# A batched inner product: larger loads, another order of the loads, and a new way of giving them to the two queues

## The chip, the cores and the metric

The kernel runs on one core of one Trainium2 chip. The metric is the device time in microseconds (us): the median of three runs of the kernel before was 49.61 us (49.56 to 49.82). The profile is of a single execution; its span, 47.8 us, leaves out a little of what the device time counts.

## The reference

Two inputs of 32 matrices each are multiplied element by element, and each product is summed to one number:

```python
x, y: (32, 256, 256) float32
return np.einsum('bij,bij->b', x, y).astype(np.float32)   # 32 numbers
```

Each input is 8.39 MB, so 16.78 MB have to be read once; the output is 128 bytes.

## The kernel before

A matrix has 65,536 elements, 512 for each of the 128 partitions (`F = 512`). The kernel reads the inputs as a flat row of numbers and cuts it in blocks of three sizes. A **single** is one matrix (256 KB for x, rows of 2 KB in each partition). A **pair** is two matrices (512 KB, rows of 4 KB): the first 64 partitions hold the first one. A **slab** is four matrices (1 MB, rows of 8 KB), 32 partitions for each. At the end there are **halves** of a single: half of the columns (128 KB, rows of 1 KB). Each block is loaded twice, once from x and once from y.

The order in the program is: singles 0 and 1, pair 1, slabs 1 to 4, pairs 10 to 14, then matrices 30 and 31 in two halves each. A function per size (`load_single`, `load_pair`, `load_slab`, `load_half`) takes the next of two DMA queues in turn, SyncE's (`nc.sync`, SP in the profile, queue q1) and ScalarE's (`nc.scalar`, ACT, queue q10), issues the load of x and then of y on it, and calls `ttr`.

`ttr` (line 81) is one VectorE instruction that multiplies the two tiles, throws the products away into `junk`, and sums each partition's products into one column of an accumulator: `acc_slab`, `acc_pair` or `acc_one`. A short second instruction reads the accumulated value out. The second half of a matrix begins with the sum of the first half (`chain=True`).

The sum over partitions is left to TensorE: a matmul of the accumulator with a mask of ones for the right partitions (lines 142, 158 and 175). VectorE copies each result from PSUM to SBUF (lines 150, 166, 177), and small transfers bring it to the output (line 151 for slabs, 167 and 170 for pairs, 178 and 179 for singles and halves).

The framework orders the work. Each tile pool gives its buffers out in turn (`SLAB_BUFS = 4`, `PAIR_BUFS = 4`, `SM_BUFS = 6`), and a load into a buffer in use waits until VectorE has read it. Loads also take eight completion semaphores, DMAHW0 to DMAHW7, in turn; a load waits on its queue until the transfer that last used its semaphore has landed. Each queue issues its transfers in order, so a load that waits holds up the loads behind it.

Of the kernel before, what the change touches and what calls it, by code (L numbers as in the profile page):

```python
# [9 lines left out]
SLAB = 4  # L10
SLAB_BUFS = 4
PAIR_BUFS = 4
SM_BUFS = 6


@with_exitstack
def kernel(
    ctx: ExitStack,
    tc: tile.TileContext,
    x: bass.AP,  # L20
    y: bass.AP,
    out: bass.AP,
):
    nc = tc.nc
    P = nc.NUM_PARTITIONS

    B, M, N = x.shape
    E = M * N
    F = E // P

    x_flat = x.rearrange("b i j -> (b i j)")
    y_flat = y.rearrange("b i j -> (b i j)")

    def grouped(flat, nb):
        return flat.rearrange("(u p f) -> u p f", p=P, f=nb * F)

    x_slab = grouped(x_flat, SLAB)
    y_slab = grouped(y_flat, SLAB)
    x_pair = grouped(x_flat, 2)
    y_pair = grouped(y_flat, 2)  # L40
    x_one = grouped(x_flat, 1)
    y_one = grouped(y_flat, 1)

    n_slabs = 4
    n_pairs = 6
    assert 2 + 2 + n_slabs * SLAB + 5 * 2 + 2 == B

    slab_pool = ctx.enter_context(tc.tile_pool(name="slab", bufs=SLAB_BUFS))
    pair_pool = ctx.enter_context(tc.tile_pool(name="pair", bufs=PAIR_BUFS))
    sm_pool = ctx.enter_context(tc.tile_pool(name="sm", bufs=SM_BUFS))  # L50
    singles_pool = ctx.enter_context(tc.tile_pool(name="singles", bufs=1))
    psum_pool = ctx.enter_context(tc.tile_pool(name="psum", bufs=1, space=bass.MemoryType.PSUM))

    acc_slab = singles_pool.tile([P, n_slabs], mybir.dt.float32)
    acc_pair = singles_pool.tile([P, n_pairs], mybir.dt.float32)
    acc_one = singles_pool.tile([P, 4], mybir.dt.float32)
    junk = singles_pool.tile([P, SLAB * F], mybir.dt.float32)

    lanes = P // SLAB
    mask_slab = singles_pool.tile([P, SLAB], mybir.dt.float32)  # L60
    nc.vector.memset(mask_slab[:], 0.0)  # L61
    for q in range(SLAB):
        nc.vector.memset(mask_slab[q * lanes : (q + 1) * lanes, q : q + 1], 1.0)  # L63
    mask_pair = singles_pool.tile([P, 2], mybir.dt.float32)
    nc.vector.memset(mask_pair[:], 0.0)
    nc.vector.memset(mask_pair[0:64, 0:1], 1.0)
    nc.vector.memset(mask_pair[64:128, 1:2], 1.0)
    ones = singles_pool.tile([P, 1], mybir.dt.float32)
    nc.vector.memset(ones[:], 1.0)

    rings = [nc.sync, nc.scalar]
    ring_idx = 0

    def next_ring():
        nonlocal ring_idx
        eng = rings[ring_idx % 2]
        ring_idx += 1
        return eng

    def ttr(x_ap, y_ap, acc_ap, chain=False):  # L80
        nc.vector.tensor_tensor_reduce(  # L81
            out=junk[:, : x_ap.shape[-1]],
            in0=x_ap,
            in1=y_ap,
            scale=1.0,
            scalar=(acc_ap if chain else 0.0),
            op0=mybir.AluOpType.mult,
            op1=mybir.AluOpType.add,
            accum_out=acc_ap,
        )  # L90

    def load_single(b, col):
        eng = next_ring()
        x_tile = sm_pool.tile([P, F], mybir.dt.float32, name="x_s")
        y_tile = sm_pool.tile([P, F], mybir.dt.float32, name="y_s")
        eng.dma_start(out=x_tile[:], in_=x_one[b])
        eng.dma_start(out=y_tile[:], in_=y_one[b])
        ttr(x_tile[:], y_tile[:], acc_one[:, col : col + 1])

    def load_half(b, h, col, chain):  # L100
        H = F // 2
        eng = next_ring()
        x_tile = sm_pool.tile([P, H], mybir.dt.float32, name="x_h")
        y_tile = sm_pool.tile([P, H], mybir.dt.float32, name="y_h")
        eng.dma_start(out=x_tile[:], in_=x_one[b][:, h * H : (h + 1) * H])
        eng.dma_start(out=y_tile[:], in_=y_one[b][:, h * H : (h + 1) * H])
        ttr(x_tile[:], y_tile[:], acc_one[:, col : col + 1], chain=chain)

    def load_pair(u, col):
        eng = next_ring()  # L110
        x_tile = pair_pool.tile([P, 2 * F], mybir.dt.float32, name="x_p")
        y_tile = pair_pool.tile([P, 2 * F], mybir.dt.float32, name="y_p")
        eng.dma_start(out=x_tile[:], in_=x_pair[u])
        eng.dma_start(out=y_tile[:], in_=y_pair[u])
        ttr(x_tile[:], y_tile[:], acc_pair[:, col : col + 1])

    def load_slab(u, col):
        eng = next_ring()
        x_tile = slab_pool.tile([P, SLAB * F], mybir.dt.float32, name="x_b")
        y_tile = slab_pool.tile([P, SLAB * F], mybir.dt.float32, name="y_b")  # L120
        eng.dma_start(out=x_tile[:], in_=x_slab[u])
        eng.dma_start(out=y_tile[:], in_=y_slab[u])
        ttr(x_tile[:], y_tile[:], acc_slab[:, col : col + 1])

    load_single(0, 0)
    load_single(1, 1)
    load_pair(1, 0)
    for i in range(n_slabs):
        load_slab(1 + i, i)
    load_pair(10, 1)  # L130
    load_pair(11, 2)
    load_pair(12, 3)
    load_pair(13, 4)
    load_pair(14, 5)
    load_half(30, 0, 2, False)
    load_half(30, 1, 2, True)
    load_half(31, 0, 3, False)
    load_half(31, 1, 3, True)

    res_slab_psum = psum_pool.tile([n_slabs, SLAB], mybir.dt.float32)  # L140
    for q in range(SLAB):
        nc.tensor.matmul(  # L142
            res_slab_psum[:, q : q + 1],
            acc_slab[:],
            mask_slab[:, q : q + 1],
            start=True,
            stop=True,
        )
    res_slab_sbuf = singles_pool.tile([n_slabs, SLAB], mybir.dt.float32)
    nc.vector.tensor_copy(out=res_slab_sbuf[:], in_=res_slab_psum[:])  # L150
    nc.sync.dma_start(
        out=out[4 : 4 + n_slabs * SLAB].rearrange("(c q) -> c q", q=SLAB),
        in_=res_slab_sbuf[:],
    )

    res_pair_psum = psum_pool.tile([n_pairs, 2], mybir.dt.float32)
    for g in range(2):
        nc.tensor.matmul(  # L158
            res_pair_psum[:, g : g + 1],
            acc_pair[:],  # L160
            mask_pair[:, g : g + 1],
            start=True,
            stop=True,
        )
    res_pair_sbuf = singles_pool.tile([n_pairs, 2], mybir.dt.float32)
    nc.vector.tensor_copy(out=res_pair_sbuf[:], in_=res_pair_psum[:])  # L166
    nc.scalar.dma_start(
        out=out[2:4].rearrange("(c g) -> c g", g=2), in_=res_pair_sbuf[0:1]
    )
    nc.scalar.dma_start(  # L170
        out=out[20:30].rearrange("(c g) -> c g", g=2), in_=res_pair_sbuf[1:6]
    )

    res_one_psum = psum_pool.tile([4, 1], mybir.dt.float32)
    nc.tensor.matmul(res_one_psum[:], acc_one[:], ones[:], start=True, stop=True)  # L175
    res_one_sbuf = singles_pool.tile([4, 1], mybir.dt.float32)
    nc.vector.tensor_copy(out=res_one_sbuf[:], in_=res_one_psum[:])  # L177
    nc.sync.dma_start(out=out[0:2], in_=res_one_sbuf[0:2, 0])
    nc.sync.dma_start(out=out[30:32], in_=res_one_sbuf[2:4, 0])


# [28 lines left out]
```

## Time and profile before

| what | value |
|---|---|
| time, median of 3 | 49.61 us |
| span of the profiled execution | 47.8 us |
| moved by DMA | 16.79 MB, mean 351 GB/s |
| VectorE busy | 20.6 us (43%), 44 instructions |
| TensorE busy | 0.8 us (2%) |
| ScalarE busy with computing | none |
| product of a slab, pair, single, half | 2.29, 1.23, 0.69, 0.43 to 0.49 us |
| issue of the last load; of the last output | 42.07; 45.69 us |

The page shows the span in 40 slices of 1.19 us each; a digit is the busy share of a slice in tenths. A line of the timeline begins with the start in us and the duration, then engine, line, operation and tiles; engines with a q (SPq, ACTq) are the queues' issuing instructions. A line of the stretches has the busy time and count of instructions of TensorE, its weight load, VectorE and GpSimd, then TensorE's clock, the DMA share and GB/s.

### The profile page before, as it was taken

Reading aid. Unit: us, or ns where it says so; the run is one execution under the profiler, and the core shown is the slowest. Engines: PE = TensorE matmul, PEld = TensorE weight load, DVE = VectorE, ACT = ScalarE, POOL = GpSimd, SP = SyncE. Lnnn points to the kernel's source line nnn. Section 1 sums busy time; section 2 is a strip of 40 time slices with the busy share of each in tenths; the row PEclk is TensorE's granted clock in tenths of the full one; section 3 lists DMA queues with packets and bytes.
Section 4 is the critical chain, followed back from the end, with each engine's and each line's share of the span. In section 5 each row is a group of like instructions: output and inputs, shape, how many; then the busy total and the mean of one; then the engine's idle time right before and its main releaser. Section 6 shows DMA issues by size and latency. Waiting matters only on the chain.

```text
span 47.8 us, 176 instructions
## 1 busy us (share of the span) xinstructions
PE 0.8 (2%) x14; PEld 0.5 (1%) x14; DVE 20.6 (43%) x44; POOL 0.2 (0%) x4
## 2 busy tenths in 40 slices
PE   0000000000000000000000000002000000001100
PEld 0000000000000000000000000002000000001000
DVE  2100005051900494008901970899254549199700
POOL 1000000000000000000000000000000000000000
DMA  0689999999999999999999999999999999994000
GB/s 0 103 285 434 381 417 412 415 443 432 418 418 412 412 432 439 419 412 432 412 408 436 391 439 395 405 412 412 401 422 391 424 395 398 354 323 119 0 0 7
DMA packets 4637, 16.79 MB, mean 351 GB/s; under 512 B 540, under 2 KB 1564, under 8 KB 3612
## 3 DMA queue, kind: packets, MB, share of 16 engines
q10 hardware_dynamic: 2316, 8.39, 44.9%
q1 hardware_dynamic: 2320, 8.39, 44.2%
q14 instruction: 1, 0.01, 0.0%
HBM read 16.78 MB, written 0.00 MB: 351 GB/s over the span
## 4 chain that ended last, share of the span: by engine, by line
DMA 84%; issue 5%; DVE 4%; PE 0%
DMA y_b<-in_y_dram 33%; DMA x_p<-in_x_dram 28%; DMA y_p<-in_y_dram 12%; DMA x_s<-in_x_dram 11%; DVE junk L81 3%; DVE acc_one L81 1%; PE res_one_psum L175 0%; DVE res_one_sbuf L177 0%; DVE acc_pair L81 0%; DVE res_pair_sbuf L166 0%
## 5 line engine op out<-in xcount | busy, mean ns | idle before, releaser
L81 DVE CUSTOM_DVE_ANT_0 junk<-x_b,y_b 128x2048 f32<-128x2048 f32 x4 | 9.2, 2292 | 10.1 <-DMA y_b<-in_y_dram 6.9
L81 DVE CUSTOM_DVE_ANT_0 junk<-x_p,y_p 128x1024 f32<-128x1024 f32 x6 | 7.4, 1225 | 5.6 <-DMA y_p<-in_y_dram 4.5
L81 DVE CUSTOM_DVE_ANT_0 junk<-x_s,y_s 128x512 f32<-128x512 f32 x2 | 1.4, 692 | 7.7 <-DMA y_s<-in_y_dram 7.7
L81 DVE CUSTOM_DVE_ANT_0 junk<-x_h,y_h,acc_one 128x256 f32<-128x256 f32 x2 | 1.0, 485 | 0.0
L81 DVE CUSTOM_DVE_ANT_0 junk<-x_h,y_h 128x256 f32<-128x256 f32 x2 | 0.9, 426 | 0.1
L142 PE MATMUL res_slab_psum<-mask_slab,acc_slab 128*4 128x1 f32 x8 | 0.3, 164 | 32.4 <-DVE acc_slab L81 32.4
L142 PEld LDWEIGHTS res_slab_psum<-mask_slab,acc_slab 128*4 128x4 f32 x8 | 0.2, 83 | 32.4 <-DVE acc_slab L81 32.4
L81 DVE DVE_READ_ACCUMULATOR2_ANT acc_pair<- 128x1 f32 x6 | 0.5, 83 | 0.0
L81 DVE DVE_READ_ACCUMULATOR2_ANT acc_one<- 128x1 f32 x6 | 0.5, 83 | 0.0
L158 PE MATMUL res_pair_psum<-mask_pair,acc_pair 128*6 128x1 f32 x4 | 0.2, 164 | 10.2 <-DVE acc_pair L81 10.2
L61 DVE MEMSET mask_slab<- 128x4 f32 x1 | 0.1, 62 | 0.8 <-PEq L194 0.8
L81 DVE DVE_READ_ACCUMULATOR2_ANT acc_slab<- 128x1 f32 x4 | 0.3, 82 | 0.0
L63 DVE MEMSET mask_slab<- 32x1 f32 x4 | 0.2, 59 | 0.1
L177 DVE COPY res_one_sbuf<-res_one_psum 4x1 f32<-4x1 f32 x1 | 0.1, 145 | 0.3 <-PE res_one_psum L175 0.3
L158 PEld LDWEIGHTS res_pair_psum<-mask_pair,acc_pair 128*6 128x6 f32 x4 | 0.1, 86 | 10.3 <-DVE acc_pair L81 10.3
L175 PE MATMUL res_one_psum<-ones,acc_one 128*4 128x1 f32 x2 | 0.2, 165 | 1.8 <-DVE acc_one L81 1.8
L150 DVE COPY res_slab_sbuf<-res_slab_psum 4x4 f32<-4x4 f32 x1 | 0.1, 145 | 0.0
L166 DVE COPY res_pair_sbuf<-res_pair_psum 6x2 f32<-6x2 f32 x1 | 0.1, 143 | 0.0
L175 PEld LDWEIGHTS res_one_psum<-ones,acc_one 128*4 128x4 f32 x2 | 0.1, 84 | 1.9 <-DVE acc_one L81 1.9
L194 POOL MEMSET const-bfloat16-1.0<- 128x1 bf16 x1 | 0.1, 101 | 0.0
L194 POOL MEMSET const-uint8-127<- 128x1 uint8 x1 | 0.1, 101 | 0.0
L194 POOL MEMSET const-float32-0.0<- 128x1 f32 x1 | 0.1, 98 | 0.2 <-issue 0.2
(5 smaller groups left out, 0.3 us busy)
## 6 DMA issues: line engine op xcount, KB each, us to landing
x_b<-in_x_dram ACTq DMA_DIRECT2D x2, 1024.0 KB, 5.6
x_b<-in_x_dram SPq DMA_DIRECT2D x2, 1024.0 KB, 13.7
y_b<-in_y_dram SPq DMA_DIRECT2D x2, 1024.0 KB, 18.2
y_b<-in_y_dram ACTq DMA_DIRECT2D x2, 1024.0 KB, 9.7
x_p<-in_x_dram SPq DMA_DIRECT2D x3, 512.0 KB, 16.4
y_p<-in_y_dram SPq DMA_DIRECT2D x3, 512.0 KB, 9.5
x_p<-in_x_dram ACTq DMA_DIRECT2D x3, 512.0 KB, 13.1
y_p<-in_y_dram ACTq DMA_DIRECT2D x3, 512.0 KB, 15.6
```

The costliest lines, as they stand in the source:

```text
L61: nc.vector.memset(mask_slab[:], 0.0)
L63: nc.vector.memset(mask_slab[q * lanes : (q + 1) * lanes, q : q + 1], 1.0)
L81: nc.vector.tensor_tensor_reduce(out=junk[:, : x_ap.shape[-1]], in0=x_ap, in1=y_ap, scale=1.0, scalar=(acc_ap if chain else 0.0), op0=mybi ...
L142: nc.tensor.matmul(res_slab_psum[:, q : q + 1], acc_slab[:], mask_slab[:, q : q + 1], start=True, stop=True,)
L150: nc.vector.tensor_copy(out=res_slab_sbuf[:], in_=res_slab_psum[:])
L158: nc.tensor.matmul(res_pair_psum[:, g : g + 1], acc_pair[:], mask_pair[:, g : g + 1], start=True, stop=True,)
L166: nc.vector.tensor_copy(out=res_pair_sbuf[:], in_=res_pair_psum[:])
L175: nc.tensor.matmul(res_one_psum[:], acc_one[:], ones[:], start=True, stop=True)
L177: nc.vector.tensor_copy(out=res_one_sbuf[:], in_=res_one_psum[:])
L194: nc = _bacc.Bacc("TRN2", target_bir_lowering=False, num_devices=1)
```

## The change

The change loads most of the input in the largest block. The inputs are cut in six slabs (matrices 0 to 23), two pairs (24 to 27), two singles (28 and 29) and the four halves as before (30 and 31), in this order from large to small, so that the small pieces stand at the end and little work is left after the last one. Blocks are given to the queue that has fewer bytes so far (`pick_ring`), with the first two slabs fixed to one queue each; the function for these is called `load_slab_quarters`, but it loads whole slabs just as `load_slab` does. The copies of the slab and pair results from PSUM move from VectorE to ScalarE, and the outputs, now in one piece for each accumulator, need one transfer each: three in place of five. `SM_BUFS` goes from 6 to 8. The masks, the products and the matmuls are the same.

In the built program SyncE's queue has slabs 0, 2 and 4, and ScalarE's slabs 1, 3 and 5, then one pair, one single and two halves each. ScalarE's two copies, with a load of its function table ahead of the first, stand behind all loads of its queue. SyncE's queue ends with the slab output, which waits for the first of these copies, and the output of singles and halves. SyncE's loads use the even semaphores and ScalarE's the odd ones.

```diff
-SM_BUFS = 6
+SM_BUFS = 8
...
-    acc_slab = singles_pool.tile([P, n_slabs], mybir.dt.float32)
-    acc_pair = singles_pool.tile([P, n_pairs], mybir.dt.float32)
+    n_slab_cols = 6
+    acc_slab = singles_pool.tile([P, n_slab_cols], mybir.dt.float32)
+    acc_pair = singles_pool.tile([P, 2], mybir.dt.float32)
...
-    def next_ring():
-        nonlocal ring_idx
-        eng = rings[ring_idx % 2]
-        ring_idx += 1
-        return eng
+    ring_bytes = [0, 0]
+
+    def pick_ring(nbytes, forced=None):
+        if forced is None:
+            i = 0 if ring_bytes[0] <= ring_bytes[1] else 1
+        else:
+            i = forced
+        ring_bytes[i] += nbytes
+        return rings[i]
...
+    def load_slab_quarters(u, col, ring_i):
+        eng = pick_ring(2 * FS * P * 4, forced=ring_i)
+        x_tile = slab_pool.tile([P, FS], mybir.dt.float32, name="x_b")
+        y_tile = slab_pool.tile([P, FS], mybir.dt.float32, name="y_b")
+        eng.dma_start(out=x_tile[:], in_=x_slab[u])
+        eng.dma_start(out=y_tile[:], in_=y_slab[u])
+        ttr(x_tile[:], y_tile[:], acc_slab[:, col : col + 1])
...
-    load_single(0, 0)
-    load_single(1, 1)
-    load_pair(1, 0)
-    for i in range(n_slabs):
-        load_slab(1 + i, i)
-    load_pair(10, 1)
-    load_pair(11, 2)
-    load_pair(12, 3)
-    load_pair(13, 4)
-    load_pair(14, 5)
+    load_slab_quarters(0, 0, 0)
+    load_slab_quarters(1, 1, 1)
+    load_slab(2, 2)
+    load_slab(3, 3)
+    load_slab(4, 4)
+    load_slab(5, 5)
+    load_pair(12, 0)
+    load_pair(13, 1)
+    load_single(28, 0)
+    load_single(29, 1)
     load_half(30, 0, 2, False)
     load_half(30, 1, 2, True)
     load_half(31, 0, 3, False)
     load_half(31, 1, 3, True)
...
-    nc.vector.tensor_copy(out=res_slab_sbuf[:], in_=res_slab_psum[:])
+    nc.scalar.copy(out=res_slab_sbuf[:], in_=res_slab_psum[:])
     nc.sync.dma_start(
-        out=out[4 : 4 + n_slabs * SLAB].rearrange("(c q) -> c q", q=SLAB),
+        out=out[0 : n_slab_cols * SLAB].rearrange("(c q) -> c q", q=SLAB),
         in_=res_slab_sbuf[:],
     )
...
-    nc.vector.tensor_copy(out=res_pair_sbuf[:], in_=res_pair_psum[:])
+    nc.scalar.copy(out=res_pair_sbuf[:], in_=res_pair_psum[:])
     nc.scalar.dma_start(
-        out=out[2:4].rearrange("(c g) -> c g", g=2), in_=res_pair_sbuf[0:1]
-    )
-    nc.scalar.dma_start(
-        out=out[20:30].rearrange("(c g) -> c g", g=2), in_=res_pair_sbuf[1:6]
+        out=out[24:28].rearrange("(c g) -> c g", g=2), in_=res_pair_sbuf[:]
     )
...
-    nc.sync.dma_start(out=out[0:2], in_=res_one_sbuf[0:2, 0])
-    nc.sync.dma_start(out=out[30:32], in_=res_one_sbuf[2:4, 0])
+    nc.sync.dma_start(out=out[28:32], in_=res_one_sbuf[:, 0])
```

## The prediction

> **What bounds the kernel now.** I read the page's slices first, for the limiting resource.
>
> ```profile
> span 47.8 us, 176 instructions
> DVE  2100005051900494008901970899254549199700
> DMA  0689999999999999999999999999999999994000
> ```
>
> From slice 3 (3.6 us) to slice 35 (43.0 us) the transfers run at nine tenths or more, while VectorE (DVE) is busy for 43% of the span. The 16.78 MB of input set the time. A change can then win only in the rate of the transfers, in the start, or in the tail after the last byte. So next come stretches of the trace (the last two columns are DMA share and GB/s):
>
> ```profile
> 2.50:3.00 0.50, 0.00 (x0) 0.00 (x0) 0.00 (x0) 0.00 (x0) 1.00 0.43 123
> ...
> 15.00:20.00 5.00, 0.00 (x0) 0.00 (x0) 2.30 (x2) 0.00 (x0) 1.00 1.02 426
> ...
> 30.00:35.00 5.00, 0.34 (x8) 0.24 (x8) 3.60 (x5) 0.00 (x0) 1.00 1.03 410
> 35.00:40.00 5.00, 0.00 (x0) 0.00 (x0) 3.02 (x5) 0.00 (x0) 1.00 1.02 402
> ...
> 42.50:43.00 0.50, 0.02 (x1) 0.02 (x2) 0.47 (x3) 0.00 (x0) 1.00 0.90 283
> 43.00:43.50 0.50, 0.23 (x4) 0.12 (x4) 0.50 (x4) 0.00 (x0) 1.00 0.78 184
> 43.50:44.00 0.50, 0.00 (x0) 0.00 (x0) 0.47 (x3) 0.00 (x0) 1.00 0.28 94
> ```
>
> Slabs (8 KB rows) move at about 425 GB/s, pairs (4 KB rows) at 402 to 410, and the rate falls away over the last 1.5 us. The queue view for 43.0 to 44.2 us says why:
>
> ```profile
> DMA packets 160, 0.14 MB, mean 116 GB/s; under 512 B 24, under 2 KB 160, under 8 KB 160
> q10 hardware_dynamic: 160, 0.14, 44.2%
> ```
>
> Only one queue has work: the other has delivered its last half, and ScalarE's queue is alone with a half that it issued late. The timeline shows the finish:
>
> ```profile
> 41.69 1.23 DVE L81 CUSTOM_DVE_ANT_0 junk<-x_p,y_p 128x1024 f32<-128x1024 f32 x1 [1.01 <-issue]
> 42.07 0.33 ACTq L106 DMA_DIRECT2D y_h<-in_y_dram  x1
> 44.43 0.48 DVE L81 CUSTOM_DVE_ANT_0 junk<-x_h,y_h,acc_one 128x256 f32<-128x256 f32 x1
> 45.38 0.27 SPq L178 DMA_DIRECT2D out_dram<-res_one_sbuf  x1
> 45.69 0.27 SPq L179 DMA_DIRECT2D out_dram<-res_one_sbuf  x1
> ```
>
> The last y half is issued at 42.07 us and lands 2.0 us later (issue view), at 44.07. From 41.69 us DVE works almost without a break: a pair that landed late and four halves, done at 44.92 us. Then matmul, copy and two output transfers one after the other; the span ends 2.1 us after the second one's issue (47.8 - 45.69).
>
> **What the Trainium skill says.** *DMA: Bandwidth & Descriptors*, "Queues, rings and completion order": each of the 16 engines takes turns between the queues that have work for it, packet by packet. The trace agrees: between 13 and 20 us, with slabs on both queues, each delivered 1.50 MB; between 25 and 30 us, slab rows against pair rows, 1.29 against 0.76 MB. Equal rows make the queues advance in lockstep. Same page, "Where 436 GB/s comes from": a ceiling of 435 GB/s for the core; the 426 above is 98% of it, so slabs have no rate left to gain. *ScalarE: Activation LUTs*, "What ACT_TABLE_LOAD costs": about 1283 ns, or 2.66 us with its drain. No instruction of this kernel computes on ScalarE, so the trace has no row for it.
>
> **The change part by part.**
>
> *Fewer, larger loads.* Slabs go from 4 to 6 (8.39 to 12.58 MB), pairs from 6 to 2 (6.29 to 2.10 MB); singles (1.05 MB) move from first to near the end; halves (1.05 MB) stay last. I lay the new bytes along the measured rates. At 5.0 us the half-microsecond stretches sum to 1.06 MB; at 425 GB/s that is a start at 5.0 - 2.5 = 2.5 us, ramp included. I keep 2.5, since the first transfer on ScalarE's queue is a slab in both versions. Then:
> - slabs 12.58 / 0.425 = 29.6 us, until 32.1
> - pairs 2.10 / 0.406 (mean of 402 and 410) = 5.2, until 37.3
> - singles: no stretch has them alone. Between the pairs' 406 and the halves' 361 GB/s (41 to 42 us), I take 390: 2.7, until 40.0
> - halves 1.05 / 0.36 = 2.9, until 42.9.
>
> The same sum for the kernel before: 2.5 + 8.39/0.425 + 6.29/0.406 + 2.7 + 2.9 = 43.3 us, where its last half landed at 44.07. So larger rows are worth 0.4 us, and 0.8 us were lost in the tail, where one queue ran dry.
>
> *The tail of the queues.* Loads take eight completion semaphores in turn, and a load waits until the last user of its semaphore has landed. In the built program before, the two queues wait on each other's semaphores (ScalarE's last y half on DMAHW0, SyncE's on DMAHW6), so ScalarE's last issue comes at 42.07. Afterwards SyncE has the even semaphores and ScalarE the odd, four loads deep each. The last y half waits for the y single of its own queue, which lands at about 40.0 + 0.3. Behind it then lie three halves per queue, 0.79 MB in all, 2.2 us of work. Issue to first data takes about 1.2 us (first issue 0.72 us; 66 GB/s in 1.5 to 2.0), so no queue runs dry. I charge 0.4 us for landing and uneven engines: last landing at 43.3, not 44.07. Bounds: no charge, 42.9; the full 0.8 us again, 43.7.
>
> *The new wait.* The fifth and sixth slab reuse the buffers of the first two, so their issue waits for DVE. Slab 1 is complete at 2.5 + 4.19/0.425 = 12.4 us; two products of 2.37 us (spacing 30.04 to 32.41) end near 15.1 and 17.5. Behind that issue on its queue are all later loads, but each queue still holds the x and y of slabs 2 or 3, until 22.3 us. At least 4.8 us of slack: cost nothing.
>
> *DVE.* Lockstep brings slabs in twos, the last two at 32.1 + 0.5 = 32.6. Work from there, by spacings in the timeline: 2 x 2.37 (slabs) + 2 x 1.27 (pairs, 41.69 to 42.96) + 2 x 0.74 (singles, 692 ns and the accumulator read) + 1.95 (halves, 42.96 to 44.92) = 10.7, until 43.3 at the earliest. The data path says 43.3 + 0.97 (two halves landing together) = 44.3. DVE is close, but the data decides: 44.3 against 44.92, a gain of 0.6 us.
>
> *ScalarE copies.* Two copies of PSUM leave DVE (145 ns each; the slab one is off the path, the pair one delayed the halves by about 0.1). On ScalarE they stand behind all its loads, with a table load first. Its last load goes at 40.3 to 40.7 us; plus 0.33 issue, plus 1.28 to 2.66, plus two copies of about 0.2 (estimate; DVE's take 0.145), ends at 42.4 to 44.1. SyncE's slab output waits for the first copy, and behind it stands only the final output, due at 44.3 + 0.46 = 44.8 (before: 44.92 to 45.38). I take 1.28; both ends are hidden behind the last halves.
>
> *Outputs.* The two final transfers become one: SyncE's second issue, 45.69 - 45.38 = 0.31 us, is gone from the path. The joined pair output goes earlier than the final one: nothing.
>
> Sum: 0.6 + 0.3 = 0.9 to 1.0 off 49.61, so **48.6 us**. With the tail's bounds, 43.7 instead of 43.3 gives 49.0, 42.9 gives 48.2.
>
> **The rivals.**
> - *DVE becomes the bound.* For it: the last two slab products (4.7 us) fill nearly all of the 5.2 us that the pairs take to arrive, and only 1.0 us separates the two paths. Against: DVE's average is 43%. If the last slabs land at 34 instead of 32.6 us, DVE ends at 34 + 10.7 = 44.7; with one output less, 0.2 + 0.3 gained: 49.1. With 34.5, 49.6.
> - *Slower: lockstep costs rate, or the table load comes out last.* Before, an x slab always ran beside a y slab or pair; now x runs beside x and y beside y, 1 MB apart, which no stretch shows. At 395 GB/s the slabs take 31.8 us, 2.2 more: 48.6 + 2.2 = 50.8; at 410, 49.7. If ScalarE's last load goes at 42.07 as before, then 42.4 + 2.66 + 0.4 = 45.5 is the pair output's issue, which ends near 47.8 with its wait: no gain, 49.8. Together I call it 50.1. Against: rate was 410 or more in every mixture of rows of 4 KB or more.
> - *A better start too.* The dip to 123 GB/s at 2.5 us comes while one queue carries 2 KB rows. If slabs on both queues avoid it, 0.5 us more: 48.1. Against: the first slab was in flight in the dip and did not fill it.
>
> **How the numbers follow.** Forecast 0.60; DVE as bound 0.14; slower 0.16; better start 0.10. Range: the forecast with its bounds (48.2 to 49.0), down to the better start at 48.0, up to 49.7 for the DVE case and the 410 GB/s form of the third. Faster by over 0.5% (below 49.36): 0.60 + 0.10, and a part of the DVE case, 0.74. Same: the rest of the DVE case and the mildest of the slower one, 0.11. Slower: 0.15.
>
> **What would show it.** Right: transfers at about 425 GB/s until 32 us; both queues delivering until 43 us; last issues of halves before 41 us; last product ending near 44.3; ScalarE's table load between 40.5 and 43.5; one final output about 0.5 us after the last product. Wrong: a slab rate below 415, DVE without a gap from 33 us on, a ScalarE copy later than the last product, or one queue silent in the last microsecond again.

## The result and the profile after

| | time, median | range of the runs | profiled span |
|---|---|---|---|
| before | 49.70 us (15 runs) | 49.56 to 49.82 | 47.8 us |
| after | 49.22 us (12 runs) | 49.00 to 49.41 | 47.4 us |

The ratio is 0.9903 (95% interval 0.9883 to 0.9924): about 0.5 us faster, half of the 1.0 us that was forecast. The time lies in the stated range, and the direction was right; the size was not. The runs of the new kernel are spread over 0.4 us, those of the old one over 0.26. Here and below, medians and ranges are of all runs, while ratios, intervals and mean spans leave out the five runs of three kernels (run e1, e9 and e16) that are marked slow.

The page of the kernel after, the same three lines:

```profile
span 47.4 us, 165 instructions
...
DVE  2100000000069992000299960000899959897710
...
DMA  0689999999999999999999999999999999994000
```

The transfers fill the same slices as before. VectorE has its products in bursts of two now, as blocks come in twos. In the stretches the columns are those of before, with one for ScalarE (ACT) ahead of GpSimd:

```profile
30.00:35.00 5.00, 0.00 (x0) 0.00 (x0) 1.69 (x1) 0.00 (x0) 0.00 (x0) 1.00 1.02 413
35.00:40.00 5.00, 0.35 (x8) 0.25 (x8) 4.43 (x7) 0.00 (x0) 0.00 (x0) 1.00 1.04 398
...
42.00:43.00 1.00, 0.00 (x0) 0.00 (x0) 0.96 (x4) 0.69 (x3) 0.00 (x0) 1.00 1.09 344
...
43.00:43.50 0.50, 0.00 (x0) 0.00 (x0) 0.46 (x3) 0.00 (x0) 0.00 (x0) 1.00 0.27 78
```

The last full microsecond moves 344 GB/s, and at 43.5 us all is read; before, the rate faded from 42.5 to 44.0. The queue view for 42.5 to 43.3 us has both queues, as forecast:

```profile
q1 hardware_dynamic: 147, 0.13, 52.2%
q10 hardware_dynamic: 88, 0.07, 29.9%
```

ScalarE's queue has read its last bytes at 42.9 us and SyncE's at 43.3. In the kernel before it was 42.8 for SyncE's and 43.8 for ScalarE's.

So the last data comes earlier, and yet little of it is left in the timeline:

```profile
41.02 0.33 SPq L128 DMA_DIRECT2D y_h<-in_y_dram  x1
...
41.21 1.28 ACT L156 ACT_TABLE_LOAD   x1 [41.21 <-DVE acc_pair L78]
...
42.50 0.15 ACT L156 COPY res_slab_sbuf<-res_slab_psum 6x4 f32<-6x4 f32 x1
...
42.68 0.35 SPq L157 DMA_DIRECT2D out_dram<-res_slab_sbuf  x1
...
43.92 0.43 DVE L78 CUSTOM_DVE_ANT_0 junk<-x_h,y_h 128x256 f32<-128x256 f32 x1 [0.33 <-DMA y_h<-in_y_dram]
...
44.39 0.48 DVE L78 CUSTOM_DVE_ANT_0 junk<-x_h,y_h,acc_one 128x256 f32<-128x256 f32 x1
...
45.34 0.28 SPq L181 DMA_DIRECT2D out_dram<-res_one_sbuf  x1
```

The last half on SyncE's queue lands at 43.77 us (41.02 plus 2.75 in the chain of waits), 0.3 us before the last landing of the old kernel. But VectorE was idle and starts 0.15 us later, and two products stand behind it: its own and that of the other last half, which landed on ScalarE's queue at about 43.4 us (40.84 + 2.6) but comes second in the program. The last product ends at 44.88 us, where it ended at 44.92. The output is issued at 45.34 in place of 45.38. What is left is the second final output: the last issue was at 45.69 and is at 45.34 now. From there to the end it is 2.0 us, before 2.1.

One trace settles this only to some 0.2 us. In a second trace of the same kernel (`e0_after_again` below) the last half on SyncE's queue lands 0.2 us earlier, and the last product and the output follow:

```profile
44.20 0.48 DVE L78 CUSTOM_DVE_ANT_0 junk<-x_h,y_h,acc_one 128x256 f32<-128x256 f32 x1
...
45.15 0.28 SPq L181 DMA_DIRECT2D out_dram<-res_one_sbuf  x1
```

Here the output is issued 0.54 us before the last one of the old kernel: 0.31 are the second output, 0.23 come from the data. The traced run of the kernel before, at 49.55 us, was also faster than all 15 timed ones.

One part lies outside the span. Each run gives the device time and the span. Over all runs of the kernel before, the time is 1.80 us above the span, and over those of the kernel after 1.92 us. So 0.12 us of the gain in the span is lost outside it.

### The profile page after: what moved, and what is told of

Read it like the earlier page. It is cut to its first block, busy times and chain, and to the rows that moved or that the text cites. A ratio compares the mean times of both kernels' runs of the same rounds, so it can differ in the third digit from the quotient of the medians.

```text
span 47.4 us, 165 instructions
## 1 busy us (share of the span) xinstructions
PE 0.8 (2%) x14; PEld 0.5 (1%) x14; DVE 20.1 (43%) x38; ACT 1.5 (3%) x3; POOL 0.2 (0%) x4
## 4 chain that ended last, share of the span: by engine, by line
DMA 84%; issue 6%; DVE 2%; SPq 2%; PE 0%; DVEq 0%
DMA y_b<-in_y_dram 61%; DMA y_s<-in_y_dram 17%; DMA y_h<-in_y_dram 6%; DVE junk L78 2%; SPq L93 1%; SPq L101 1%; PE res_one_psum L178 0%; DVE res_one_sbuf L180 0%; DVE acc_one L78 0%; DVE acc_slab L78 0%; DVEq L78 0%
## 5 line engine op out<-in xcount | busy, mean ns | idle before, releaser
L78 DVE CUSTOM_DVE_ANT_0 junk<-x_b,y_b 128x2048 f32<-128x2048 f32 x6 | 13.8, 2292 | 22.7 <-DMA y_b<-in_y_dram 22.6
L78 DVE CUSTOM_DVE_ANT_0 junk<-x_p,y_p 128x1024 f32<-128x1024 f32 x2 | 2.5, 1226 | 0.5 <-DMA y_p<-in_y_dram 0.5
L156 ACT ACT_TABLE_LOAD x1 | 1.3, 1283 | 41.2 <-DVE acc_pair L78 41.2
```

The costliest lines, as they stand in the source:

```text
L78: nc.vector.tensor_tensor_reduce(out=junk[:, : x_ap.shape[-1]], in0=x_ap, in1=y_ap, scale=1.0, scalar=(acc_ap if chain else 0.0), op0=mybi ...
L156: nc.scalar.copy(out=res_slab_sbuf[:], in_=res_slab_psum[:])
```

## The experiments

Theory A: the gain is the removed output, and the loads bring almost nothing, since what the data gains is lost again behind the last landing. Theory B: the loads bring it. Others are named where they come up. Every ratio is to the kernel before, timed on the same chip; there were four chips, on which the kernel before had medians of 49.63 us (e0 to e4), 49.76 (e5 to e8), 49.78 (e9 to e12) and 49.70 (e13 to e16). These ratios are not those of the medians; the two differ by up to 0.003.

**The change again, and with two final outputs.**

> The changed kernel itself, as the measure for the others on the same chip. Ratio to the kernel before 0.990, as measured: 0.988 to 0.993.

Measured: 49.24 us, ratio 0.992 (0.9895 to 0.9946), span 47.3 in the median.

```diff
-    nc.sync.dma_start(out=out[28:32], in_=res_one_sbuf[:, 0])
+    nc.sync.dma_start(out=out[28:30], in_=res_one_sbuf[0:2, 0])
+    nc.sync.dma_start(out=out[30:32], in_=res_one_sbuf[2:4, 0])
```

> The changed kernel with its last output in two transfers again, one after the other on SyncE's queue. Theory A (the gain is nearly all the removed final transfer; earlier data is lost again behind the last landing): 0.31 us longer than the changed kernel, ratio to the kernel before 0.996 to 1.000. Theory B (the loads bring the gain, and the output's landing time hides the second one): ratio stays at 0.990 to 0.992.

Measured: 49.40 us, ratio 0.995 (0.9932 to 0.9967), span 47.5. The second output costs 0.16 to 0.2 us, less than the 0.31 of theory A and more than the nothing of theory B. In its one trace (of an execution of 50.01 us) the second issue follows the first after 0.32 us (45.88 to 46.20), but from the last issue to the end it is 1.88 us, where it is 2.00 in the trace with one output; that leaves a cost of 0.2. It seems that 0.2 to 0.3 us come from the rest of the change; the intervals of the two kernels overlap.

**The outputs alone.** The kernel before keeps its sizes, order and queues. Only the matrices in the blocks are exchanged, so that each accumulator's results stand together in the output.

```diff
-    load_single(0, 0)
-    load_single(1, 1)
-    load_pair(1, 0)
+    load_single(28, 0)
+    load_single(29, 1)
+    load_pair(13, 5)
     for i in range(n_slabs):
-        load_slab(1 + i, i)
+        load_slab(i, i)
...
+        out=out[16:28].rearrange("(c g) -> c g", g=2), in_=res_pair_sbuf[:]
...
-    nc.sync.dma_start(out=out[0:2], in_=res_one_sbuf[0:2, 0])
-    nc.sync.dma_start(out=out[30:32], in_=res_one_sbuf[2:4, 0])
+    nc.sync.dma_start(out=out[28:32], in_=res_one_sbuf[:, 0])
```

> The kernel before with its own load sizes and order of queues, but other matrices given to the blocks so that each accumulator's output is one transfer; copies stay on VectorE. Theory A: 0.3 to 0.4 us faster, ratio 0.992 to 0.994. Theory B: ratio 0.998 to 1.000.

Measured: 49.15 us, ratio 0.9893 (0.9866 to 0.9921), span 47.35. Three outputs in place of five give as much as the whole change, with the sizes, the order and the queues of the loads as before; that is more than theory A expected (0.992 to 0.994). Its final issue and the product before it, in the timeline:

```profile
44.31 0.49 DVE L81 CUSTOM_DVE_ANT_0 junk<-x_h,y_h,acc_one 128x256 f32<-128x256 f32 x1
...
45.27 0.28 SPq L175 DMA_DIRECT2D out_dram<-res_one_sbuf  x1
```

Of its 0.45 us of span, 0.42 are the last issue (45.69 to 45.27): 0.31 are the second issue and 0.1 a product that ends earlier. A second trace of this kernel (`e14_dealt_before_sizes` below) has the last product end at 44.90 us, as in the kernel before, and the last issue at 45.37, so only the 0.31 stand in both. The time was 0.47 to 0.48 us shorter than that of the kernel before on both chips; where the other 0.16 come from is not shown. The edit also joins the two pair outputs and gives the blocks other matrices, and neither was tried alone.

**One product less behind the last landing.** All loads of x go on SyncE's queue, all of y on ScalarE's, so that blocks are complete one by one.

```diff
-        eng.dma_start(out=x_tile[:], in_=x_slab[u])
-        eng.dma_start(out=y_tile[:], in_=y_slab[u])
+        nc.sync.dma_start(out=x_tile[:], in_=x_slab[u])
+        nc.scalar.dma_start(out=y_tile[:], in_=y_slab[u])
```

(and likewise for pairs, singles and halves)

> The changed kernel with every x load on SyncE's queue and every y load on ScalarE's, so that blocks are complete one by one and not in twos. Theory A (two halves complete together at the end, so two products of 0.48 us stand behind the last landing): one product leaves the tail, 0.4 to 0.5 us less than the changed kernel, ratio 0.980 to 0.983. Theory C (VectorE works without a break at the end and is itself the bound, whenever the data lands): no change from 0.990.

Measured: 48.85 us, ratio 0.9832 (0.9805 to 0.986), span 46.95. The timeline shows only one product behind the last landing:

```profile
43.39 0.42 DVE L78 CUSTOM_DVE_ANT_0 junk<-x_h,y_h 128x256 f32<-128x256 f32 x1 [0.22 <-DMA x_h<-in_x_dram]
...
44.04 0.48 DVE L78 CUSTOM_DVE_ANT_0 junk<-x_h,y_h,acc_one 128x256 f32<-128x256 f32 x1 [0.22 <-DMA x_h<-in_x_dram]
```

The last data lands no earlier (41.23 + 2.64 = 43.88 us), but the product before it is done by then. VectorE is idle ahead of both, so it is not itself the bound here: theory C falls. The same kernel on another chip:

> The x and y kernel once more, beside the next three on one chip. If its 0.4 us over the changed kernel is its own and not the chip's: ratio 0.981 to 0.986, span 46.9 to 47.1 us, last product without another one behind it.

Measured: 49.42 us (48.99 to 49.73), ratio 0.9911 (0.9886 to 0.9937), span 47.5. The gain of 0.981 to 0.986 was not there. The product is alone at the end in this trace too, but it comes late, as the stretches show:

```profile
42.00:43.00 1.00, 0.00 (x0) 0.00 (x0) 0.82 (x5) 0.99 (x3) 0.00 (x0) 1.00 0.89 243
43.00:44.00 1.00, 0.00 (x0) 0.00 (x0) 0.75 (x4) 0.04 (x1) 0.00 (x0) 1.00 0.61 161
```

Transfers are under way (share 0.89 and 0.61) but move only 243 and 161 GB/s, against 302 and 84 in the first run: some reads take far longer than the others. Twelve after 40 us take over 200 ns, up to 589, where most reads of 1 KB take 47. (In the first run there were twelve as well, up to 308 ns.) In the timeline VectorE sits idle for 0.86 us ahead of its last product; the last half lands at 44.64 us:

```profile
44.80 0.48 DVE L78 CUSTOM_DVE_ANT_0 junk<-x_h,y_h,acc_one 128x256 f32<-128x256 f32 x1 [0.86 <-DMA x_h<-in_x_dram]
```

**The copies on VectorE.**

```diff
-    nc.scalar.copy(out=res_slab_sbuf[:], in_=res_slab_psum[:])
+    nc.vector.tensor_copy(out=res_slab_sbuf[:], in_=res_slab_psum[:])
...
-    nc.scalar.copy(out=res_pair_sbuf[:], in_=res_pair_psum[:])
+    nc.vector.tensor_copy(out=res_pair_sbuf[:], in_=res_pair_psum[:])
```

In the x and y kernel, twice, and in the changed kernel:

> The kernel with x on one queue and y on the other (ratio 0.983), its two early copies from PSUM back on VectorE, so that ScalarE loads no table. Prediction's account (both homes of the copies are hidden): 0.981 to 0.985. Rival (ScalarE's 1.28 us table load and the slab output behind it are worth something, or VectorE's two copies of 0.145 us delay the last products): off by 0.1 us or more either way, ratio under 0.981 or over 0.985.

> The x and y kernel with its two early copies on VectorE, once more. If the copies are hidden in both homes, its span is that of the x and y kernel within 0.1 us, and what its time has more stands outside the span (2.0 to 2.1 us in place of 1.9). If the copies or their early outputs delay the last loads, the span is 0.3 us longer, as in its first run.

> The changed kernel with its two early copies on VectorE and no table load on ScalarE, blocks dealt to the queues as in the change. Hidden in both homes: span 47.2 to 47.4 us as in the changed kernel, ratio 0.988 to 0.994. If ScalarE's copies helped the last products: 0.15 to 0.3 us slower, ratio 0.994 to 0.998. If the table load held back the end: ratio under 0.987.

Measured: x and y kernel 49.38 us, 0.9907 (0.9874 to 0.9939), and 49.38 us, 0.9915 (0.9885 to 0.9946), span 47.3 both times; changed kernel 49.27 us, 0.9896 (0.9864 to 0.9928), span 47.2. In the changed kernel no cost of either home is seen, but the two were measured on different chips. The ratios of the x and y kernel lie outside the expected 0.981 to 0.985; against its first run, which was on another chip, no statement can be made. Beside its second run (span 47.5) the copies on VectorE cost nothing. All three have more time outside the span, 2.02 to 2.08 us against 1.91 to 1.93 with the copies on ScalarE.

The second x and y run and the last two kernels here were timed on one chip (e9 to e12), so they can be compared for their queues too: with the new sizes, x and y on two queues (49.42 and 49.38 us) are no faster than the dealing of the change (49.27 us). The trace of the x and y kernel with copies on VectorE shows again a last half that came late:

```profile
44.38 0.49 DVE L78 CUSTOM_DVE_ANT_0 junk<-x_h,y_h,acc_one 128x256 f32<-128x256 f32 x1 [0.65 <-DMA x_h<-in_x_dram]
```

**Rows of the last loads.** In the x and y kernel, singles for the last two matrices, or for matrix 30 only:

```diff
-    load_half(30, 0, 2, False)
-    load_half(30, 1, 2, True)
-    load_half(31, 0, 3, False)
-    load_half(31, 1, 3, True)
+    load_single(30, 2)
+    load_single(31, 3)
```

> The kernel with x and y on two queues, matrices 30 and 31 loaded as singles (rows of 2 KB) in place of halves (1 KB). Theory D (rows of 1 KB move at 350 GB/s and so make the end late): last landing 0.3 to 0.4 us earlier, the last product 0.2 longer, 0.1 to 0.2 us faster, ratio 0.979 to 0.981. Theory E (the last us before the last landing is a fixed fading-out of 16 engines that end at different times, whatever the rows): last landing unchanged, 0.2 us slower, ratio 0.986 to 0.988.

> The kernel with x and y on two queues, matrix 30 as a single and only matrix 31 in halves. Theory D: half of the cost of the small rows goes, the last product stays short: 0.15 to 0.2 us faster than with four halves, ratio 0.979 to 0.980. Theory E: no change, 0.982 to 0.984.

Measured: singles 48.95 us, 0.983 (0.9794 to 0.9867), span 47.15; one single and two halves 49.36 us, 0.9912 (0.9881 to 0.9943), also with a span of 47.15, but 2.19 us outside it. The stretches of the kernel with singles:

```profile
41.00:42.00 1.00, 0.00 (x0) 0.00 (x0) 0.63 (x2) 0.00 (x0) 0.00 (x0) 1.00 1.05 385
42.00:43.00 1.00, 0.00 (x0) 0.00 (x0) 0.31 (x3) 0.00 (x0) 0.00 (x0) 1.00 0.93 336
43.00:44.00 1.00, 0.00 (x0) 0.00 (x0) 0.61 (x3) 0.00 (x0) 0.00 (x0) 1.00 0.03 10
```

Rows of 2 KB move at 385 GB/s where rows of 1 KB moved at 344 in the same microsecond of the first x and y run. By 43 us only 0.01 MB is left, in place of 0.08. The last landing is at 43.69 us (chain of waits), 0.2 us earlier than in that run, and the product is 0.2 longer, so the net is nothing. Theory D is right on the rate but not on its worth: the landing moved by half of what it expected. Theory E's fading-out is there with both row sizes. Two limits: that first run was on another chip, while on the chip of these runs the kernel with four halves (copies on VectorE) took 49.38 us with a span of 47.3, so there the kernel with singles was the faster one; and the kernel with one single and two halves met neither expectation.

**The sizes of before, x and y on two queues.** This is the kernel with the outputs alone, with the edit of the queues.

> The load sizes and order of the kernel before (singles first, four slabs, six pairs, four halves), three outputs, but x on SyncE's queue and y on ScalarE's. It differs from the x and y kernel in sizes, order and the home of the copies. Prediction's account (larger rows are worth 0.4 us): ratio 0.990 to 0.992. Theory A (sizes and order are worth nothing at the end, only outputs and the last products count): 0.982 to 0.985.

> The load sizes and order of the kernel before, x and y on two queues, three outputs, once more. Theory A (sizes and order are worth nothing): equal to the x and y kernel within 0.1 us of span. Prediction's account: 0.3 us or more longer.

Measured: 48.79 us, 0.9806 (0.9766 to 0.9847), and 48.77 us, 0.9812 (0.9784 to 0.984), span 47.0 both times. The old sizes are as good as the new, or better.

**Sizes and dealing, two by two on one chip.**

> One of four kernels on one chip, all with three outputs and copies on VectorE: load sizes of the change, blocks dealt to the queues in turn. Prediction's account (sizes bring 0.4 us): span 0.3 to 0.4 us under the kernel with sizes of before in the same dealing. Theory A (what the data gains is lost to two products behind the last landing): within 0.1 us of it, ratio 0.988 to 0.992.

> Second of the four: load sizes and order of before, dealt in turn, so that ScalarE's queue is alone in the last us. Ratio 0.988 to 0.992, as in its first run. If a queue that runs dry costs the 0.8 us (or the 0.4) of the prediction, 0.4 to 0.8 us longer than the fourth kernel; theory A: 0.2 to 0.35 us longer.

> Third of the four: sizes of the change, x on one queue and y on the other. Theory A alone: 0.4 us under the first kernel. If the sizes of the change themselves bring stalls of the last halves (as in two of this kernel's traces): spread of 0.4 us between its runs, and no better than the first kernel in the median.

> Fourth of the four: sizes and order of before, x on one queue and y on the other. Ratio 0.980 to 0.983 and little spread, as twice before. Prediction's account: 0.3 to 0.4 us longer than the third kernel; theory A: the shortest of the four, or equal to the third.

| three outputs, copies on VectorE | dealt in turn | x and y on two queues |
|---|---|---|
| sizes of the change: time | 49.44 us, 0.9941 (0.9916 to 0.9966) | 49.16 us, 0.9876 (0.9842 to 0.9911) |
| span (mean), outside it | 47.4; 2.06 us | 47.1; 2.05 us |
| sizes of before: time | 49.23 us, 0.9891 (0.986 to 0.9921) | 48.93 us, 0.9819 (0.9783 to 0.9855) |
| span (mean), outside it | 47.5; 1.79 us | 47.2; 1.77 us |

By the medians (49.70 us before on this chip) the four ratios would be 0.995, 0.989, 0.991 and 0.985, in the same order. In the span, the sizes are worth 0.1 us or less in both columns, and the queues 0.3 us in both rows. In the time, the new sizes lose 0.2 us, all of it outside the span.

The two rows are not equally sure. With the sizes of before, the ratio is 0.989 dealt in turn (two runs) and 0.981 to 0.982 with x and y on two queues (three runs). With the new sizes and copies on VectorE it is 0.990 and 0.994 dealt in turn, and 0.991, 0.992 and 0.988 with x and y on two queues: the 0.3 us of this chip was not there on the one before. The timelines of the upper row, dealt first:

```profile
44.00 0.43 DVE L78 CUSTOM_DVE_ANT_0 junk<-x_h,y_h 128x256 f32<-128x256 f32 x1 [0.33 <-DMA y_h<-in_y_dram]
44.47 0.48 DVE L78 CUSTOM_DVE_ANT_0 junk<-x_h,y_h,acc_one 128x256 f32<-128x256 f32 x1
```

and with x and y on two queues:

```profile
43.40 0.43 DVE L78 CUSTOM_DVE_ANT_0 junk<-x_h,y_h 128x256 f32<-128x256 f32 x1 [0.26 <-DMA x_h<-in_x_dram]
44.06 0.48 DVE L78 CUSTOM_DVE_ANT_0 junk<-x_h,y_h,acc_one 128x256 f32<-128x256 f32 x1 [0.22 <-DMA x_h<-in_x_dram]
```

Their last landings are at 43.84 and 43.90 us, nearly equal; the product that no longer stands behind it is the 0.4 us between these two traces. In the lower row the reason is another. Dealt in turn, VectorE has no pause from the last pair on:

```profile
41.69 1.23 DVE L81 CUSTOM_DVE_ANT_0 junk<-x_p,y_p 128x1024 f32<-128x1024 f32 x1 [1.00 <-DVE acc_pair L81]
42.05 0.33 ACTq L106 DMA_DIRECT2D y_h<-in_y_dram  x1
...
44.42 0.48 DVE L81 CUSTOM_DVE_ANT_0 junk<-x_h,y_h,acc_one 128x256 f32<-128x256 f32 x1
```

The last half lands at 44.1 us (42.05 + 2.1) and waits 0.3 us for VectorE. What sets the end is the last pair, from 41.69 us, with 3.2 us of products from there on. VectorE stands idle for 1.0 us ahead of it; the profile names no load for this wait. With x and y on two queues that product began at 41.15, 41.11 and 41.52 us in the three runs of that kernel, in the first of them with its wait for a load named:

```profile
41.15 1.23 DVE L81 CUSTOM_DVE_ANT_0 junk<-x_p,y_p 128x1024 f32<-128x1024 f32 x1 [1.17 <-DMA x_p<-in_x_dram]
```

In the first two the end is then set by the last landing (43.85 us in the first) and one product; in the third, on this chip, the chain from the pair still has no pause and ends 0.16 us earlier than dealt in turn. The kernel before has the shape of the dealt one: pair at 41.69, last product done at 44.92.

## Why the prediction was right in part and wrong in size

- **Larger rows, 0.4 us: right until 40 us, and of little use at the end.** The stretches of the kernel after sum to 15.70 MB by 40.0 us, where the sum of rates had 15.73. The kernel before had 15.58 by then, so the new sizes led by 0.3 us. At the end of the products 0.04 us is left in one trace and 0.23 in the other, and the two-by-two shows 0.1 us or less in the span.
- **The tail of the queues, 0.8 us charged down to 0.4: this step failed.** It put the last landing at 43.3 us, and it came at 43.77 (43.87 in the second trace): of the 0.6 us that the data was to bring, 0.47 are lost in this term, and most of the rest in the 0.15 us until VectorE starts, named below. The step read the 0.8 us between the sum of rates and the last landing of the kernel before as the loss of a queue that ran dry. There one queue was alone for the last 1.0 us (42.8 to 43.8); in the kernel after it was alone for 0.4 (42.9 to 43.3), and the same gap stands: 42.9 by the sum, 43.77 measured, the upper bound of 43.7 and not 43.3. The terms are rows of 1 KB at 357, 345 and 344 GB/s (40 to 43 us), with the fading-out 3.3 us for the last 1.08 MB in place of 2.9, and 0.45 us from the last bytes to the landing. The step also passed over what the prediction had seen in the timeline: in the kernel before VectorE works almost without a break from 41.69 us on, and the last half waits 0.3 us for it, so there the chain from the last pair sets the end, and not that landing.
- **Two products behind the landing, 0.97 us: right** (0.96), but for 0.15 us from the landing to VectorE's start. What was missed is that this is new. Before, the last landing was followed by about 0.8 us, and it is followed by 1.1 us now. The 0.3 us that the data gained in this trace are lost in these terms.
- **Outputs, 0.31 us: right, and the main term.** The outputs alone gave 0.9893 and 0.9891, as much as the whole change, and would have made the direction right by themselves. But the parts don't add up: the same outputs are worth 0.47 to 0.48 us with the loads of before and only 0.16 to 0.2 us with those of the change. Only a part of this is explained, by the shorter end after two outputs.
- **The sum.** 0.62 and 0.31 us are 0.93; the forecast of 48.6 rounds this up to 1.0. This is small beside the miss.
- **ScalarE: right.** The table load took 1283 ns, the figure of the Trainium skill, *ScalarE: Activation LUTs*, "What ACT_TABLE_LOAD costs"; the drain of 1380 ns that it adds is not in this trace, as the copy begins 0.01 us after the load ends (41.21 + 1.28 to 42.50). Table load, copies and the issue of the slab output end at 43.0 us, 2.3 us ahead of the final output's issue.
- **The wait for slab buffers: right.** Slab 5's loads were issued at 18.06 us, 5 us before the queue's older ones had landed (23.05).
- **Rivals.** Lockstep did not cost rate: 419 to 431 GB/s for slabs in the kernel after, 5 to 30 us. DVE was not the bound over the last 10 us. A better start did not come: 1.05 MB by 5.0 us, against 1.06 before.
- **Outside the span, +0.12 us: not thought of,** and its cause is open. It goes with the program (1.77 to 2.19 us over all kernels here), not with the chip. The traces hold one thing that goes along with it, a packet of 8 KB on an instruction queue (q14). In the six traces with the sizes of before it comes at 46.1 to 46.8 us, within the span, and 1.77 to 1.81 us lie outside. In the five with the sizes of the change and copies on VectorE it comes at 48.8 to 49.4 us, after the end of the span, and 2.02 to 2.08 us lie outside. In the seven others none is recorded after the start; 1.91 to 1.93 us lie outside for five of them, 1.81 and 2.19 for the two with matrix 30 as a single. That it is the cause is not shown.

Two things stay open: what makes single reads among the last halves take much longer in some runs (with 243 and 161 GB/s as the sign), and why most kernels with the new sizes spread over 0.4 to 0.9 us from run to run. Neither was tried further. The traces give a hint on the first: after 40 us, five of the eight with x and y on two queues and four halves have 8 to 12 reads of over 200 ns, and none of the eight dealt in turn has more than two. So the queues of x and y may themselves bring on the late halves that undo their gain; no run tests it.

## What to carry to other kernels

When transfers bound a kernel, look at its end from both sides: what lands last, and what still has to be computed after each of the last landings. A gain in the first is lost if two blocks now land together. Put the two operands of a product on the two queues, so that blocks are complete one by one, and join small outputs that go out one after another at the end: here these two edits alone, with the loads in their old sizes and order, gave 0.981 to 0.982 in three runs on three chips, better than the change. With the new sizes, the two queues helped on two chips of three. And test the cheapest part of a change by itself before its name gets the gain.

## What was not expected of the hardware

- Rows of 8, 4, 2 and 1 KB moved at about 424, 406, 385 and 345 GB/s, with a DMA share of 1.0 or more in each case; the figure for 2 KB is from one microsecond of one run.
- The Trainium skill, *DMA: Bandwidth & Descriptors*, "Issuing engines are not separate DMA queues", says that issuing from several engines saves only issue time. The rates here agree (a slab stream has 419 to 434 GB/s over 5 us in either dealing), but which loads share a queue sets the order of completion. That was worth 0.3 us of the span with the sizes of before, and 0.4, 0.3 and nothing on three chips with the new ones.
- At the end of the loads it was 0.3 to 0.5 us from the last bytes to the last landing, 0.44 of it in the one trace whose last rows have 2 KB.
